# FFN down-projections as 2x2 block products in seven multiplications, summed over all block pairs in four PSUM banks

## The chip, the cores and the metric

One core of a Trainium2 chip runs the whole program. The metric is the time on the device in microseconds; shown are the median of three runs and the range, and one execution with a profile.

## The reference

A decoder trunk of two layers on `x` of 1024 rows by 1024 columns, in fp32. Layer 0 is a retention layer, layer 1 differential attention over keys and values that are projected once from the output of layer 0; each is followed by a ConvFFN with D_FF = 2816:

```python
def conv_ffn(xn, w_up, conv_w, conv_b, w_down):
    h = xn @ w_up                        # 1024 x 5632
    ...                                  # causal depthwise conv, width 3
    g, u = jnp.split(hc, 2, axis=-1)
    return (jax.nn.silu(g) * u) @ w_down # (1024 x 2816) @ (2816 x 1024)
...
h = conv_ffn(rms_norm(x, ffn_norm_pre[layer]), ...)
x = x + rms_norm(h, ffn_norm_post[layer])
```

The change concerns the last product, once in each layer.

## The kernel before

All large products keep fp32 accuracy by a split: a tile is rounded to fp32r (`hi`, a copy on ScalarE, L82), and the rest `lo` = tile − `hi` is taken on VectorE (L83); a product is then three matmuls, hi·hi, hi·lo and lo·hi (L98 to L100 in `mm3`, L511 in `gated`).

The stages follow one another on TensorE: retention to 0.5 ms, its gated output projection, FFN up of layer 0 (about 890 to 1342 us), FFN down of layer 0 (1342 to 1608), attention (1651 to 2120) with its output projection, FFN up of layer 1 (2200 to 2632) and FFN down of layer 1 (2633 to 2881).

FFN up (`ffn_up`) is already done as 2x2 block products in seven multiplications; its operands are split through a ring of eight 128x512 tiles `wc`. After convolution and SwiGLU each of the 22 blocks of 128 features goes to DRAM (`acts[f]`, 128 features by 1024 rows).

FFN down (`gated`) reads these blocks and those of `w_down` again (`load_w`: 512 KB, 128x1024, split into a tile `hl`), in groups of 1, then nine times 2, then 3 blocks. For each group and each of 8 blocks of 128 output rows it multiplies into a PSUM tile `ps` of two banks (128x1024), of which four rotate, and VectorE adds the tile to `acc` in SBUF (copy at L527, add at L529, last group L568). That is 22 blocks x 8 row blocks x 2 column halves x 3 = 1056 matmuls of 128x512 per layer.

With the last group the generator `finish` runs over the row blocks: mean square (ScalarE L110), reciprocal root (POOL L104, L105), gain (VectorE L169), residual (L173), and in layer 0 the normed rows for attention (ScalarE L205 `xhn`), their transposes (TensorE L121) and their split (`into_xt`). The first projections of attention (keys, queries, values of head pair 0) stand between the last transposes; their weights are loaded ahead and multiplied by a gain on POOL (L90).

The order of instructions on each engine is set by the program's text and a scheduler that works from it; loads are issued by SyncE (SP) in the order in which the text asks for them.

Of the kernel before, what the change touches and what calls it, by code (L numbers as in the profile page):

```python
# [50 lines left out]
def trunk(ctx: ExitStack, tc: tile.TileContext, A, out):  # L51
# [88 lines left out]
    def into_xt(ps, sb, xt):  # L140
        c, b = divmod(sb, 4)
        cols = slice(b * P, (b + 1) * P)
        if isinstance(xt, Staged):
            xt.put(ps, c, cols)
            return
        xh, xl = xt
        split_to(xh[c][:, :, cols], xl[c][:, :, cols], ps)

    def finish(mm, add, pool, psp, gpost, x_old, x_new, xt, order=tuple(range(NS)), turn_first=False, late=()):
# [82 lines left out]
        if xt is None:  # L232
            mm(NS - 1)
            halves = []
            for u in range(2):
                us = slice(u * 512, (u + 1) * 512)
                hs, t = add(NS - 1, u)
                hg = pool.tile([P, 512], F32, name="hg", tag="w4")
                halves.append((hg, t, mean_square(hs, D)))
                nc.vector.tensor_tensor(out=hg, in0=hs, in1=gpost[:, us], op=ALU.mult)  # L240
            r = small.tile([P, 1], F32, name="rstd")
            nc.gpsimd.tensor_scalar(out=r, in0=halves[0][2], scalar1=EPS, scalar2=halves[1][2],  # L242
                                    op0=ALU.add, op1=ALU.add)
# [254 lines left out]
    def gated(wk, up, n_blk, w_down, fin):  # L498
# [21 lines left out]
        def down(first, acts, ids, ws=None):  # L520
            ws = ws or [load_w(wk.hlp, w_down[i]) for i in ids]
# [12 lines left out]
        for gi, g in enumerate(sizes):  # L534
            ids = list(range(f, f + g))
            f += g
            acts, ws = [], []
            for u, i in enumerate(ids):
                acts.append(up(i))
                if wk.stored:  # L540
                    ws.append(load_w(wk.hlp, w_down[i]))
                if todo is not None and u == (g - 1 if wk.stored and g < 3 else 0):
                    down(*todo)
            todo = (gi == 0, acts, ids, ws)
        _, acts, ids, ws = todo
        ws = ws or [load_w(wk.hlp, w_down[i]) for i in ids]
# [29 lines left out]
    def open_mid(wk, tag, side):  # L576
        st = wk.mid = ExitStack()
        wk.accp = st.enter_context(tc.tile_pool(name="acc" + tag, bufs=8, side=side, reuse_waits="tile"))
        wk.w4 = st.enter_context(tc.tile_pool(name="w4" + tag, bufs=6, side=side, reuse_waits="tile"))
        wk.gp = st.enter_context(tc.tile_pool(name="gp" + tag, bufs=1, side=side, reuse_waits="tile"))  # L580
        open_junk(wk.gp, D)

    def open_ops(wk, tag, stored=0):
        st = wk.ops = ExitStack()
        wk.stored = stored
        wk.hlp = st.enter_context(tc.tile_pool(name="hlp" + tag, bufs=stored or 5, reuse_waits="tile"))
        if stored:
            return
        wk.actp = st.enter_context(tc.tile_pool(name="act" + tag, bufs=3, reuse_waits="tile"))
# [19 lines left out]
    def ffn_up(layer, xt, tail, w_pool, late, on_drained):  # L609
# [49 lines left out]
        ring = st.enter_context(tc.tile_pool(name=f"ring{layer}", bufs=8, reuse_waits="tile"))  # L659
# [104 lines left out]
        for f in range(NF):  # L764
# [43 lines left out]
            ready.extend(coming)  # L808
            cg = conv(f, hg)
# [22 lines left out]
    open_mid(wk, "a", "left")  # L832
# [5 lines left out]
    xt3 = []  # L838

    def last(mm, add):  # L840
        xt3.append(new_xt(xtp))
        g = load_gain(wk.gp, "gpost", A["ffn_norm_post"][0])
        return finish(mm, add, wk.w4, psp, g, x1, x2, xt3[0])
# [4 lines left out]

    acts = ffn_up(0, xt, tail, wk.hlp, None, drained)
    open_ops(wk, "f", 8)  # L850
    open_mid(wk, "f", "left")
    tail = gated(wk, stored(wk, acts), NF, rows(A["w_down"][0], NF), last)
    xt = xt3[0]

# [4 lines left out]
    gq, gkv = gains4[:, 0, :], gains4[:, 1, :]  # L859
# [29 lines left out]
    def load_v(pool, p):  # L889
        gv = gkv.rearrange("p (a k) -> p a k", a=2)  # L890
        return [load_w(pool, A["w_kv_v"][p, kh], gv[:, kh, :]) for kh in range(2)]

    wkq = [load_w(wk.hlp, A["w_kv_k"][0], gkv), load_w(wk.hlp, A["w_q"][0], gq)]
    wv = load_v(wk.hlp, 0)
    pkq = []
    for w in wkq:
        next(tail)
        pkq.append(psp.tile([P, S], F32, name="ps"))
        proj_half(pkq[-1][:, :512], w, 0)
    next(tail)  # L900
    pv = psp.tile([P, 4, 256], F32, name="ps")
    for sb in range(4):
        proj_v(pv[:, sb, :], wv, xt, sb)
    for _ in tail:
        pass
    wk.mid.close()
    qkp = qk4.enter_context(tc.tile_pool(name="qk4", bufs=2, side="right", reuse_waits="tile"))
# [17 lines left out]
    split_to(vs[0][0][:, :4, :], vs[0][1][:, :4, :], pv)  # L925
    ps_pool.close()
# [315 lines left out]
    def last(mm, add):  # L1242
        g = load_gain(wk.gp, "gpost", A["ffn_norm_post"][1])
        return finish(mm, add, wk.w4, psp, g, x3, x_out, None)

    acts = ffn_up(1, xt, tail, o5, late, drained)
    open_ops(wk, "b", 9)
    open_mid(wk, "b", "right")
    tail = gated(wk, stored(wk, acts), NF, rows(A["w_down"][1], NF), last)
    for _ in tail:  # L1250
        pass
    wk.mid.close()
    wk.ops.close()
    ps_pool.close()
# [69 lines left out]
```

## Time and profile before

| | |
|---|---|
| median of 3 runs | 2894.06 us (2892.62 to 2896.27) |
| profiled execution | 2892.49 us, span 2890.7 us |
| mean granted TensorE clock | 0.988 |
| busy in the span | TensorE 96%, VectorE 66%, ScalarE 38%, POOL 13% |

A TensorE that is busy 96% of the span leaves two sources of time: fewer matmuls, and the few places where it waits.

### The profile page before, as it was taken

Reading aid. Unit: us, or ns where it says so; the run is one execution under the profiler, and the core shown is the slowest. Engines: PE = TensorE matmul, PEld = TensorE weight load, DVE = VectorE, ACT = ScalarE, POOL = GpSimd, SP = SyncE. Lnnn points to the kernel's source line nnn. Section 1 sums busy time; section 2 is a strip of 40 time slices with the busy share of each in tenths; the row PEclk is TensorE's granted clock in tenths of the full one; section 3 lists DMA queues with packets and bytes.
Section 4 is the critical chain, followed back from the end, with each engine's and each line's share of the span. In section 5 each row is a group of like instructions: output and inputs, shape, how many; then the busy total and the mean of one; then the engine's idle time right before and its main releaser. Section 6 shows DMA issues by size and latency. Waiting matters only on the chain. (4 is left out here: it accounts for less than half of the span.)

```text
span 2890.7 us, 35455 instructions
## 1 busy us (share of the span) xinstructions
PE 2779.6 (96%) x13924; PEld 2344.9 (81%) x13924; DVE 1903.4 (66%) x2474; ACT 1098.9 (38%) x1776; POOL 372.8 (13%) x594
## 2 busy tenths in 40 slices
PE   8999999999997899999998999999989899999998
PEld 7888989888886688887887788888777788887887
DVE  4432333444448898887766587777648898887666
ACT  3323232311125344443212555555545344443212
POOL 1110111000012000000002334444421000000002
PEclk9999999999998999999999999999999999999999
DMA  4111120311222222223323323223252222224332
GB/s 142 55 48 59 38 65 27 133 69 66 81 102 88 87 96 88 82 79 138 110 90 121 122 73 80 75 68 94 86 177 100 90 100 75 86 80 160 110 102 95
DMA packets 102359, 262.89 MB, mean 91 GB/s; under 512 B 11440, under 2 KB 37040, under 8 KB 102192
## 3 DMA queue, kind: packets, MB, share of 16 engines
q1 hardware_dynamic: 72224, 210.03, 21.7%
q10 hardware_dynamic: 29968, 50.60, 5.0%
q8 instruction: 109, 1.79, 0.2%
q14 instruction: 58, 0.48, 0.0%
HBM read 193.48 MB, written 54.53 MB: 86 GB/s over the span
## 5 line engine op out<-in xcount | busy, mean ns | idle before, releaser
L511 PE MATMUL ps<-hl 128*128 128x512 f32 x2112 | 487.9, 392 | 11.5 <-DVE acc L527 3.8
L511 PEld LDWEIGHTS ps<-hl 128*128 128x128 f32 x2112 | 397.6, 189 | 100.3 <-DVE acc L527 7.3
L82 ACT ACTIVATE hl<-raw 128x1024 fp32r<-128x1024 f32 x190 | 198.7, 1056 | 625.1 <-PE ps L511 319.4
L83 DVE TENSOR_TENSOR hl<-raw,hl 128x1024 fp32r<-128x1024 f32 x190 | 239.6, 1262 | 143.2 <-ACT hl L82 142.6
L529 DVE TENSOR_TENSOR acc<-ps,acc 128x1024 f32<-128x1024 f32 x192 | 234.0, 1221 | 127.2 <-PE ps L511 126.3
L98 PE MATMUL ps<-xh,hl 128*128 128x512 f32 x592 | 233.2, 394 | 2.6 <-DVE xl L83 2.4
L99 PE MATMUL ps<-xl,hl 128*128 128x512 f32 x592 | 232.0, 392 | 3.2 <-DVE xl L83 3.2
L100 PE MATMUL ps<-xh,hl 128*128 128x512 f32 x592 | 232.2, 392 | 0.0
L104 POOL TENSOR_SCALAR rstd<-ss 128x1 f32<-128x1 f32 x127 | 56.7, 447 | 1177.3 <-ACT junk L110 1172.0
L511 PE MATMUL ps<-hl,act 128*128 128x512 f32 x768 | 178.4, 392 | 0.0
L759 DVE SCALAR_TENSOR_TENSOR hbuf<-hbuf,cw,hbuf 128x1023 f32<-128x1023 f32 x124 | 156.8, 1279 | 19.5 <-ACT hbuf L757 18.6
L511 PEld LDWEIGHTS ps<-hl,act 128*128 128x128 f32 x768 | 144.1, 189 | 29.5
L83 DVE TENSOR_TENSOR wc<-raw,wc 128x512 fp32r<-128x512 f32 x208 | 140.9, 685 | 37.0 <-ACT wc L82 37.0
L82 ACT ACTIVATE wc<-raw 128x512 fp32r<-128x512 f32 x208 | 128.6, 627 | 85.6 <-PE pb L100 77.2
L90 POOL TENSOR_TENSOR raw<-raw,gains 128x1024 f32<-128x1024 f32 x32 | 66.9, 2094 | 704.0 <-DMA raw<-in_w_kv_k 662.5
L98 PE MATMUL ps<-hl,xh 128*128 128x256 f32 x544 | 154.9, 286 | 1.8 <-ACT xh L82 1.8
L100 PE MATMUL ps<-hl,xl 128*128 128x256 f32 x544 | 155.4, 286 | 0.8 <-DVE xl L83 0.7
L99 PE MATMUL ps<-hl,xh 128*128 128x256 f32 x544 | 154.8, 285 | 0.0
L757 ACT ACTIVATE hbuf<-hbuf,cw 128x1024 f32<-128x1024 f32 x88 | 109.4, 1245 | 96.1 <-DVE hbuf L731 85.5
L1013 ACT ACTIVATE s<-s,m 128x256 f32<-128x256 f32 (+7 forms) x128 | 99.1, 774 | 101.2 <-POOL m L1012 100.8
L99 PEld LDWEIGHTS ps<-xl,hl 128*128 128x128 f32 x592 | 111.9, 189 | 26.9 <-DVE xl L83 4.1
L98 PEld LDWEIGHTS ps<-xh,hl 128*128 128x128 f32 x592 | 112.0, 189 | 26.4 <-DVE xl L83 2.6
(252 smaller groups left out, 6584.3 us busy)
## 6 DMA issues: line engine op xcount, KB each, us to landing
raw<-in_w_up SPq DMA_DIRECT2D x88, 512.0 KB, 3.5
act<-hbuf ACTq DMA_DIRECT2D x44, 512.0 KB, 2.6
raw<-act SPq DMA_DIRECT2D x44, 512.0 KB, 3.2
raw<-in_w_down SPq DMA_DIRECT2D x44, 512.0 KB, 3.5
raw<-in_w_t SPq DMA_DIRECT2D x32, 512.0 KB, 3.5
xold<-x SPq DMA_DIRECT2D x24, 512.0 KB, 5.1
raw<-in_w_v SPq DMA_DIRECT2D x16, 512.0 KB, 3.5
oret<-t ACTq DMA_DIRECT2D x32, 256.0 KB, 2.3
```

The source lines that it names most:

```text
L82: nc.scalar.activation(out=hi, in_=src, func=AF.Copy)
L83: nc.vector.tensor_tensor(out=lo, in0=src, in1=hi.bitcast(F32), op=ALU.subtract)
L90: nc.gpsimd.tensor_tensor(out=v, in0=v, in1=gain.unsqueeze(2).broadcast_to([P, gain.shape[1], n]), op=ALU.mult)
L98: nc.tensor.matmul(out, sh, mh, start=start, stop=False, skip_group_check=onto)
L99: nc.tensor.matmul(out, sh, ml, start=False, stop=False, skip_group_check=onto)
L100: nc.tensor.matmul(out, sl, mh, start=False, stop=stop, skip_group_check=onto)
L104: nc.gpsimd.tensor_scalar(out=r, in0=ss, scalar1=1.0, scalar2=eps, op0=ALU.mult, op1=ALU.add)
L511: nc.tensor.matmul(ps[:, half, :], a, ws[f][:, m, hs], start=f == 0 and n == 0, stop=f == len(ws) - 1 and n == 2)
L529: nc.vector.tensor_tensor(out=acc[sb], in0=flat(ps), in1=acc[sb], op=ALU.add)
L757: nc.scalar.activation(out=hc, in_=src, func=AF.Identity, scale=cw[:, n, 2:3], bias=cw[:, n, 3:4])
L759: nc.vector.scalar_tensor_tensor(out=hc[:, j:], in0=src[:, :S - j], scalar=cw[:, n, 2 - j:3 - j], in1=hc[:, j:], op0=ALU.mult, op1=ALU.add)
L1013: nc.scalar.activation(out=s[:, :w], in_=s[:, :w], func=AF.Exp, scale=0.125, bias=m, accum_out=l[:, c:c + 1])
```

## The change

FFN down becomes the class `Down`. Rows are cut into two halves of 512 and columns into two halves of 512; the 22 blocks of features make N = 11 pairs. For each pair the 2x2 by 2x2 product is formed by seven products P1 to P7 of 512x128 by 128x512, in place of eight. The loop over the products is the outer one: P1, P7, P5, P4, P6, P3, P2, each summed over all 11 pairs in four PSUM banks (one for each 128 rows), `px` or `py`. A step (one product, one pair) is 4 x 3 = 12 matmuls of 128x512, so a layer has 7 x 11 x 12 = 924. P5 and P3 go on top of what `px` holds, P4 on top of P7 in `py`. Only after a product is a bank copied (ScalarE) or added (VectorE) into `acc`.

Operands are loaded as halves (256 KB, rows of 2 KB), kept in SBUF as fp32 (`keep...`), combined on VectorE for P7, P5, P4 (two operations per step) and P6, P3 (one), and split through the ring `wc`. Loads are asked for 6 steps ahead, operands prepared 3 steps ahead. Rows 0 to 3 are complete after P6, so `finish` runs on them under P3 and P2; the last 4 pairs of P2 are done row block by row block, for rows 4 to 7. The last row block takes its column half 1 first. The first weights of attention (`load_first`) are asked for ahead of the last row block.

```diff
+    def minus(out, x, y):
+        nc.vector.tensor_tensor(out=out, in0=x, in1=y, op=ALU.subtract)
...
-            for u in range(2):
+            for u in (1, 0):
                 us = slice(u * 512, (u + 1) * 512)
                 hs, t = add(NS - 1, u)
...
+            if f == NF - 1:
+                down = Down(layer, acts, split_part, xt.pool)
+                for _ in range(4):
+                    down.load()
+                for _ in range(3):
+                    down.prepare()
...
+        N = NF // 2
+        ORDER = [(p, i) for p in ("P1", "P7", "P5", "P4", "P6", "P3", "P2") for i in range(NF // 2)]
+        LOADED, SPLIT = 6, 3
+        BY_ROWS = 4
...
+        def load(self):
+            p, i = self.ORDER[self.loaded]
+            a, b = self.a, self.b
+            if p == "P1":
+                self.fetch(self.a11(i), a(1, 1, i))
+                self.raw[p, i] = self.two(rawp, lambda j: b(1, 1, j), i)
+            elif p == "P7":
+                for dst, src in ((self.s(i), a(2, 1, i)), (self.t(i), b(1, 2, i)), (self.v(i), b(2, 2, i))):
+                    self.fetch(dst, src)
+            elif p == "P5":
+                self.raw[p, i] = self.halves(self.w4, a(2, 2, i), b(1, 1, i))
+            elif p == "P4":
+                self.raw[p, i] = self.halves(self.w4, a(2, 2, i), b(2, 1, i))
...
+        def prepare(self):
+            p, i = self.ORDER[self.split]
+            raw = self.raw.pop((p, i), None)
+            if p == "P1":
+                x, y = self.a11(i), raw
+            elif p == "P7":
+                d = self.w4.tile([P, 1024], F32, name="d", tag="w4")
+                x, y = d[:, COLS[0]], d[:, COLS[1]]
+                minus(x, self.a11(i), self.s(i))
+                minus(y, self.v(i), self.t(i))
+            elif p == "P5":
+                x, y = self.s(i), self.t(i)
+                nc.vector.tensor_tensor(out=x, in0=x, in1=raw[:, COLS[0]], op=ALU.add)
+                minus(y, y, raw[:, COLS[1]])
+            elif p == "P4":
+                x, y = raw[:, COLS[0]], raw[:, COLS[1]]
+                minus(self.t(i), self.v(i), self.t(i))
+                minus(y, y, self.t(i))
+            elif p == "P6":
+                x, y = self.s(i), self.t(i)
+                minus(x, x, self.a11(i))
+            elif p == "P3":
+                x, y = raw, self.v(i)
+                minus(x, x, self.s(i))
+            else:
+                x, y = self.s(i), raw
+            self.ops[p, i] = self.split_part(x), self.split_part(y)
+            self.split += 1
+        def ahead(self, p, i):
+            at = self.ORDER.index((p, i))
+            while self.loaded < min(at + 1 + self.LOADED, len(self.ORDER)):
+                self.load()
+            while self.split < min(at + 1 + self.SPLIT, len(self.ORDER)):
+                self.prepare()
+        def products(self, p, i, banks, js=range(4), onto=False):
+            (ah, al), (bh, bl) = self.ops[p, i]
+            for j in js:
+                m = slice(j * P, (j + 1) * P)
+                mm3(banks[j], ah[:, m], al[:, m], bh, bl, not onto and i == 0, i == self.N - 1, onto)
+        def full(self, p, banks, pairs=None, onto=False):
+            for i in pairs or range(self.N):
+                self.ahead(p, i)
+                self.products(p, i, banks, onto=onto)
...
+            def copy(dst, src):
+                for d, b in zip(dst, src):
+                    nc.scalar.activation(out=d, in_=b, func=AF.Copy)
+            def plus(dst, src, u=None):
+                for d, b, o in zip(dst, src, u or dst):
+                    nc.vector.tensor_tensor(out=d, in0=b, in1=o, op=ALU.add)
+            x = [self.bank_x() for _ in range(4)]
+            y = [self.bank_y() for _ in range(4)]
+            self.full("P1", x)
+            copy(c(1, 1), x)
+            self.full("P7", y)
+            copy(c(2, 2), y)
+            self.full("P5", x, onto=True)
+            plus(c(2, 2), x)
+            self.full("P4", y, onto=True)
+            plus(c(2, 1), y, c(1, 1))
+            self.full("P6", y)
+            plus(c(2, 1), y)
+            plus(c(2, 2), y)
+            copy(c(1, 2), y)
+            g = fin(self.mm, self.add)
+            self.acc, self.x = acc, x
+            self.c12 = lambda: plus(c(1, 2), x)
+            n = self.N - self.BY_ROWS
+            self.steps = [("P3", i) for i in range(self.N)] + [("P2", i) for i in range(n)]
+            return g
+        SIZES = (2, 4, 4, 4, 4)
+        def mm(self, sb):
+            if sb < 5:
+                for _ in range(self.SIZES[sb]):
+                    p, i = self.steps.pop(0)
+                    if p == "P3":
+                        self.full(p, self.x, [i], True)
+                        if i == self.N - 1:
+                            self.c12()
+                            self.on_p3()
+                    else:
+                        if i == 0:
+                            self.last = [self.bank_y() for _ in range(4)]
+                        self.full(p, self.last, [i])
+            if sb >= 4:
+                for i in range(self.N - self.BY_ROWS, self.N):
+                    self.ahead("P2", i)
+                    self.products("P2", i, self.last, [sb - 4])
+        def add(self, sb, half):
+            a = self.acc[sb]
+            if sb >= 4 and half != 1:
+                nc.vector.tensor_tensor(out=a[:, COLS[0]], in0=self.last[sb - 4], in1=a[:, COLS[0]], op=ALU.add)
+            if half is not None:
+                a = a[:, COLS[half]]
+            return a, a
...
+    def load_first():
+        first_w.extend((load_w(wk.hlp, A["w_kv_k"][0], gkv), load_w(wk.hlp, A["w_q"][0], gq), load_v(wk.hlp, 0)))
```

VectorE where FFN down of layer 0 begins (`hbuf` and `u` belong to the last block of FFN up, whose results leave PSUM at L731; `hl` are the split operands of FFN down). Before:

```order
L731 TENSOR_TENSOR hbuf_7081<-pb,u 128x512 x2
L759 SCALAR_TENSOR_TENSOR hbuf_7082<-hbuf_7081,cw,hbuf_7082 128x1023
L731 TENSOR_TENSOR hbuf_7082<-pb,u 128x512
L759 SCALAR_TENSOR_TENSOR hbuf_7082<-hbuf_7081,cw,hbuf_7082 128x1022
L83 TENSOR_TENSOR hl<-raw,hl 128x1024 x2
```

and now (L735 is the old L731, L763 the old L759, `wc` are split operands of P1):

```order
L83 TENSOR_TENSOR wc<-keepl,wc 128x512
L735 TENSOR_TENSOR hbuf_7081<-pb,u 128x512
L83 TENSOR_TENSOR wc<-raw,wc 128x512
L83 TENSOR_TENSOR wc<-keepl,wc 128x512
L83 TENSOR_TENSOR wc<-raw,wc 128x512
L83 TENSOR_TENSOR wc<-keepl,wc 128x512
L83 TENSOR_TENSOR wc<-raw,wc 128x512
L735 TENSOR_TENSOR hbuf_7082<-pb,u 128x512
```

The splits of the first three steps stand ahead of the last result of FFN up, where the first split of before stood behind it and behind two convolution steps.

VectorE between P7 and P5 of layer 0, which is new (`d` and L119 are differences, L912 the sum of P5, `wc<-d` the split of P7):

```order
L119 TENSOR_TENSOR d<-keeps 128x512
L119 TENSOR_TENSOR d<-keepvh,keeph 128x512
L83 TENSOR_TENSOR wc<-d,wc 128x512 x2
L912 TENSOR_TENSOR keeps<-keeps,raw 128x512
L119 TENSOR_TENSOR d<-keeps 128x512
L119 TENSOR_TENSOR d<-keepvl,keepl 128x512
L119 TENSOR_TENSOR keeph<-keeph,raw 128x512
L83 TENSOR_TENSOR wc<-d,wc 128x512 x4
```

Differences for later steps stand ahead of the splits of earlier ones.

VectorE near the end of FFN down of layer 0, rows 4 and 5. Before:

```order
L568 TENSOR_TENSOR acc<-ps,acc 128x1024
L169 TENSOR_TENSOR acc<-acc,gpost 128x1024
L173 SCALAR_TENSOR_TENSOR acc<-acc,rstd,xold 128x1024
L83 TENSOR_TENSOR xl_11267<-ps,xh_11265 128x8x128
L568 TENSOR_TENSOR acc<-ps,acc 128x1024
```

and now (L179 is the old L169, L183 the old L173, L1025 the add of P2; `hl` are the weights of attention):

```order
L1025 TENSOR_TENSOR acc<-py,acc 128x512
L83 TENSOR_TENSOR hl<-raw,hl 128x1024
L179 TENSOR_TENSOR acc<-acc,gpost 128x1024
L83 TENSOR_TENSOR hl<-raw,hl 128x1024
L183 SCALAR_TENSOR_TENSOR acc<-acc,rstd,xold 128x1024
L83 TENSOR_TENSOR xl_11257<-px,xh_11256 128x4x128 x2
L1025 TENSOR_TENSOR acc<-py,acc 128x512
L83 TENSOR_TENSOR hl<-raw,hl 128x1024
L179 TENSOR_TENSOR acc<-acc,gpost 128x1024
L83 TENSOR_TENSOR xl_11257<-px,xh_11256 128x4x128
L183 SCALAR_TENSOR_TENSOR acc<-acc,rstd,xold 128x1024
```

The add is half as wide, and the splits of the attention weights have moved in between.

## Rows read from the trace of the kernel before

**Rows 1.** The page: busy time (share of the span) of each engine, instructions.

```profile
PE 2779.6 (96%) x13924; PEld 2344.9 (81%) x13924; DVE 1903.4 (66%) x2474; ACT 1098.9 (38%) x1776; POOL 372.8 (13%) x594
```

**Rows 2.** FFN down of layer 0: L511's matmuls, with first and last start.

```profile
L511 PE MATMUL ps<-hl x876: 388/389/390, 1371.7 to 1570.0; 128*128 128x512 f32 x176
```

**Rows 3.** Busy us (instructions) by stretch; columns in the first line.

```profile
core 0: us, PE busy (x) PEld busy (x) DVE busy (x) ACT busy (x) POOL busy (x), PEclk, DMA share, GB/s
...
1342.00:1372.00 30.00, 25.39 (x93) 18.50 (x92) 24.91 (x23) 8.92 (x9) 0.00 (x0) 0.89 0.54 197
2632.00:2660.00 28.00, 21.07 (x83) 15.12 (x84) 22.79 (x21) 8.67 (x9) 0.00 (x0) 1.00 0.58 211
1570.00:1655.00 85.00, 69.27 (x365) 58.82 (x364) 52.19 (x53) 46.17 (x64) 37.82 (x39) 0.92 0.41 139
1060.00:1330.00 270.00, 270.00 (x1193) 223.59 (x1192) 230.18 (x299) 125.82 (x169) 0.00 (x0) 1.00 0.24 84
```

**Rows 4.** What TensorE waited for, 1342 to 1372 us.

```profile
PE ps L511 <- DVE acc L527: 1.9, 2, 1.5
PE ps L511 <- DVE hbuf L731: 1.4, 1, 1.4
PE ps L511 <- DVE hl L83: 1.3, 1, 1.3
```

**Rows 5.** What TensorE waited for, 2630 to 2662 us.

```profile
PE ps L511 <- ACT hl L82: 3.0, 2, 1.7
...
PE ps L511 <- DVE hl L83: 1.8, 2, 1.4
```

**Rows 6.** What TensorE waited for, 1572 to 1655 us.

```profile
PE ps L121 <- ACT xhn L205: 13.4, 3, 9.6
PE ps L98 <- DVE xl L83: 2.4, 1, 2.4
```

**Rows 7.** The page's groups: the 128x512 splits, busy and mean ns; POOL's gains.

```profile
L83 DVE TENSOR_TENSOR wc<-raw,wc 128x512 fp32r<-128x512 f32 x208 | 140.9, 685 | 37.0 <-ACT wc L82 37.0
L82 ACT ACTIVATE wc<-raw 128x512 fp32r<-128x512 f32 x208 | 128.6, 627 | 85.6 <-PE pb L100 77.2
L90 POOL TENSOR_TENSOR raw<-raw,gains 128x1024 f32<-128x1024 f32 x32 | 66.9, 2094 | 704.0 <-DMA raw<-in_w_kv_k 662.5
```

**Rows 8.** Timeline of VectorE in FFN up: start, duration.

```profile
1304.80 0.68 DVE L731 TENSOR_TENSOR hbuf<-pb,u 128x512 f32<-128x512 f32 x1
1305.40 0.68 DVE L83 TENSOR_TENSOR wc<-raw,wc 128x512 fp32r<-128x512 f32 x1
```

**Rows 9.** Timeline of layer 0's tail: one row's chain.

```profile
1581.68 1.41 POOL L105 TENSOR_TENSOR rstd<-rstd,mhalf 128x1 f32<-128x1 f32 x1
1583.12 1.15 ACT L205 ACTIVATE xhn<-acc,rstd 128x1024 f32<-128x1024 f32 x1 [3.00 <-POOL rstd L105]
...
1584.03 1.28 DVE L173 SCALAR_TENSOR_TENSOR acc<-acc,rstd,xold 128x1024 f32<-128x1024 f32 x1 [1.35 <-POOL rstd L105]
...
1589.84 1.06 ACT L110 ACTIVATE junk<-acc 128x1024 bf16<-128x1024 f32 x1 [1.44 <-DVE acc L568]
```

**Rows 10.** Timeline of the program's end.

```profile
2879.19 1.52 PE L511 MATMUL ps<-hl 128*128 128x512 f32 x6
...
2886.03 1.41 DVE L248 SCALAR_TENSOR_TENSOR acc<-hg,rstd,xold 128x512 f32<-128x512 f32 x2 [0.45 <-POOL rstd L244]
```

**Rows 11.** DMA, 1342 to 1372 us, in 40 slices.

```profile
GB/s 0 55 339 350 404 388 399 404 421 393 415 393 235 0 0 11 0 0 82 410 208 0 0 93 377 229 0 0 126 350 246 240 284 142 11 22 147 366 153 191
```

**Rows 12.** What TensorE waited for, 880 to 980 us.

```profile
PE pb L98 <- DVE hbuf L731: 6.7, 2, 4.5
PE pb L100 <- DVE wc L83: 4.9, 2, 4.5
```

**Rows 13.** DMA, 1372 to 1570 us, in 40 slices.

```profile
GB/s 113 180 131 187 214 3 0 170 157 97 5 103 165 156 0 0 215 196 16 0 123 194 109 0 48 170 206 0 3 191 148 84 0 105 168 156 0 0 212 32
```

More of the change, by code (lines that the diff above doesn't have):

```diff
@@ L518, in flat, with down @@
             return ps.rearrange("p a b -> p (a b)")
-        def down(first, acts, ids, ws=None):
-            ws = ws or [load_w(wk.hlp, w_down[i]) for i in ids]
+        def down(first, acts, ids):
+            ws = [load_w(wk.hlp, w_down[i]) for i in ids]
             for sb in range(NS):
@@ L607, in ret_up, with ffn @@
         return up
-    def ffn_up(layer, xt, tail, w_pool, late, on_drained):
+    def ffn(layer, xt, tail, w_pool, late, on_drained, wk, fin):
         N_PRE = 6
@@ L837, in trunk, with open_half @@
     xt = nxt
-    xt3 = []
+    xt3 = [None, None], [None, None]
+    def open_half(c):
+        for part, n in zip(xt3, "hl"):
+            part[c] = xtp.tile([P, NK, 512], F32R, name=f"x{n}{c}", tag=f"x{n}{c}")
     def last(mm, add):
-        xt3.append(new_xt(xtp))
         g = load_gain(wk.gp, "gpost", A["ffn_norm_post"][0])
-        return finish(mm, add, wk.w4, psp, g, x1, x2, xt3[0])
+        open_half(0)
+        down = mm.__self__
+        down.on_p3 = lambda: open_half(1)
+        return finish(mm, add, wk.w4, down.bank_x, g, x1, x2, xt3, late=(load_first,))
     def drained():
@@ L847, in drained, with load_v @@
         wk.ops.close()
[L849 to L853, printed above, removed]
+    first_w = []
+    def load_first():
+        first_w.extend((load_w(wk.hlp, A["w_kv_k"][0], gkv), load_w(wk.hlp, A["w_q"][0], gq), load_v(wk.hlp, 0)))
+    gq, gkv = gains4[:, 0, :], gains4[:, 1, :]
+    def load_v(pool, p):
+        gv = gkv.rearrange("p (a k) -> p a k", a=2)
+        return [load_w(pool, A["w_kv_v"][p, kh], gv[:, kh, :]) for kh in range(2)]
+    tail, order = ffn(0, xt, tail, wk.hlp, None, drained, wk, last)
+    xt = xt3
     HALF = (slice(0, 64), slice(64, 128))
@@ L886, in proj_half @@
             mm3(ps, w[:, 0, ws], w[:, 1, ws], xh[c][:, k, :], xl[c][:, k, :], k == 0, k == NK - 1)
[L889 to L899, printed above, removed]
-    next(tail)
-    pv = psp.tile([P, 4, 256], F32, name="ps")
+    pkq, pv = [], []
+    next(tail)
+    bank_x, bank_y = wk.down.bank_x, wk.down.bank_y
+    wkq, wv = first_w[:2], first_w[2]
+    for u, w in enumerate(wkq):
+        if u:
+            next(tail)
+        pkq.append(bank_y())
+        proj_half(pkq[-1], w, 0)
+    next(tail)
     for sb in range(4):
-        proj_v(pv[:, sb, :], wv, xt, sb)
+        if sb % 2 == 0:
+            pv.append(bank_y().rearrange("p (j n) -> p j n", n=256))
+        proj_v(pv[-1][:, sb % 2, :], wv, xt, sb)
     for _ in tail:
@@ L1243, in last @@
         g = load_gain(wk.gp, "gpost", A["ffn_norm_post"][1])
[L1244 to L1249, printed above, removed]
+        mm.__self__.on_p3 = lambda: None
+        return finish(mm, add, wk.w4, None, g, x3, x_out, None)
+    tail, order = ffn(1, xt, tail, o5, late, drained, wk, last)
     for _ in tail:
         pass
+    order.close()
     wk.mid.close()
+    wk.ring.close()
     wk.ops.close()
-    ps_pool.close()
+    wk.banks.close()
 def layout(inputs):
```

129 lines of the change are left out of this document (92 added, 37 removed).

## The prediction

> **What bounds the kernel now.** First the page's engine shares: TensorE is busy 2779.6 of 2890.7 us [rows 1], so a change counts by the matmuls it removes and by TensorE's waits. Then L511's matmuls in the down stage: 876 starts from 1371.7 to 1570.0 us [rows 2] are (1570.0 − 1371.7)/875 = 0.2266 us from start to start, with no wait in them; the 0.39 us that a row shows for one is its length in the pipeline, not its price. Then the windows [rows 3], where 0.2266 us per start tells what a stretch loses: 1342 to 1372 us holds 93 starts, 21.1 us, and so loses 8.9 us; 2632 to 2660 us holds 83, 18.8 us, and loses 9.2. These are the two places where FFN down takes over from FFN up. The waits name the cause: the last results of FFN up, the splits `hl` and the first copies into `acc` [rows 4, 5]. In layer 0 the granted clock is 0.89 there, in layer 1 it is 1.00 [rows 3]. Last the tail of layer 0, where TensorE waits 13.4 us for `xhn` and 2.4 us for a split [rows 6], at a mean clock of 0.92 [rows 3]. Between the levels of 2.4 GHz (1) and 1.2 GHz (one half), a mean of 0.92 over 85 us is 13.6 us at the lower; 9.6 us of that can lie in the longest wait, and in the other 4.0 half the work is lost, 2.0 us. The tail loses about 13.4 + 2.4 + 2.0 = 17.8 us.
>
> **The change part by part**, against the profiled execution's own 2892.5 us (1.8 us of it around the span of 2890.7), which is 1.6 us under the median.
>
> Matmuls: 2 x (1056 − 924) = 264 fewer, of the same shape, at 0.2266 us [rows 2]: −59.8 us.
>
> What feeds them: a step of 12 matmuls lasts 2.72 us. In P7, P5 and P4 VectorE has two differences and two splits per step, four 128x512 operations. One takes 685 ns alone [rows 7], but two neighbours in a queue start 0.60 us apart [rows 8]: 2.4 us (by the lone length 2.74 us). That is 88% of the step. In FFN up VectorE is busy 230.18 of 270 us, 85%, and TensorE has 1193 starts in those 270 us, 0.2263 us each: no loss [rows 3]. So the price is nothing as long as the orders keep VectorE from waiting for ScalarE, whose two splits of 627 ns [rows 7] are 1.25 us per step. In the order of P7 and P5 differences for later steps stand ahead of earlier splits, which covers ScalarE. If that cover is gone, it is the first rival. I take the back-to-back value, since queues are full there.
>
> The adds into `acc` disappear from the steady state: of 88 per layer over two banks remain nine rounds over four single banks. Most leave time: P5 goes onto `px` and P4 onto `py` without any read in between. P6 starts in the very banks that P4 leaves, and each has to be read by VectorE first: 0.69 us for the first, while splits of two steps stand ahead of it in that queue; the other three follow at 0.60 us, and TensorE needs 0.68 us for a bank's three matmuls. From 0.7 to 2.5 us per layer. Under P3, VectorE also holds P6's eight adds and the first rows of `finish`: 1.8 us of each 2.72 for the steps, 4.8 us of adds, 2.6 us per row (residual 1.28 [rows 9], the gain taken to be as long), which the three steps of lead can just hold. No row of before shows these. From below the price is nothing, from above 10 us per layer (a wait of the size of the longest in the tail, 9.6 us [rows 6], at one of the places). I take +5 us for both layers, nearer to the short waits of 1.3 to 1.7 us that such handovers cost in rows 4 and 5.
>
> The start of FFN down: the first three steps are split ahead of the last results of FFN up, and the first copy out of a bank comes after 11 steps, so all three waits of rows 4 and 5 have lost their cause. What is late next is the handover of PSUM from `pb` to `px`, with a read of the last product by VectorE ahead of it. I leave about 1 us each: 18.1 − 2 = −16 us (bounds 0 and −18).
>
> Tail of layer 0: rows 0 to 3 are finished under P3 and P2, so their `xhn` come early, and only rows 4 to 7 follow each other at 12 matmuls, 2.72 us. One row's chain: add 0.69 (as a split [rows 7]), square 1.06, POOL's root up to 1.41, residual 1.28, a second square and root, `xhn` 1.15 [rows 9]: up to 9.5 us with the summing and handovers left out. After the last matmul of FFN down TensorE has 24 matmuls for the keys, 24 for the queries and 96 of half width for the values, some 22 us, ahead of the first product that needs row 7. The keys need row 3's split, whose second half stands on VectorE behind row 5's residual and a weight split. Row 5's last matmul is 5.4 us before the stage's end; add 0.7, square 1.1, root 1.4, residual 1.3, a 128x1024 split that I take as long as the residual, 1.3, and the split's half 0.7 make 6.5, and with 0.3 to 2 for handovers 6.8 to 8.5: late by 1.4 to 3. On POOL the reciprocal roots stand behind the gain multiplications of the attention weights, 2.09 us each [rows 7], which wait for their loads: another 0 to 6 us if these come late. I leave 7 of 17.8 us: −11 (bounds −17 and 0).
>
> Tail of layer 1: six matmuls stand from 2879.19 for 1.52 us, to 2880.7, and VectorE's last piece ends at 2886.03 + 1.41 = 2887.4 [rows 10], 6.7 us later. Now half 1 of the last row is complete before P2, and only a half add, square, root and residual follow: −2.
>
> Loads: P7 needs three of 256 KB per step, 786 KB per 2.72 us or 290 GB/s; the other products need two at most, 193. Before, 339 to 421 GB/s lasted for ten slices of 0.75 us [rows 11], with whole 512 KB loads. I take no cost. The Trainium skill, page "DMA: Bandwidth & Descriptors", section "Bandwidth", says to batch DMAs to 1 MiB or more, since smaller ones reach less than three quarters of the peak; the change halves them. From its times for 64 KB (0.95 us) and 1 MB (6.15 us) I estimate 2.0 us for 256 KB, and 6.0 us per P7 step if the three came one by one, +72 us over 22 steps. Rows 11 speak against that rule here: several half-megabyte loads in flight ran at 339 to 421 GB/s.
>
> Start of FFN up: the ring of split operands now lies elsewhere, and the order of splits there changes a little: the splits for the X21 products come after those of two more operands. TensorE waits there 6.7 us and 4.9 us for VectorE already [rows 12]. Between 0 and +5; I take +2.5.
>
> Sum: −59.8 + 5 − 16 − 11 − 2 + 2.5 = −81.3, 2811.2 by the profiled execution, 2813 for the median.
>
> **Rivals.**
> 1. Slower: each step's chain runs without overlap, difference, ScalarE split, VectorE split. In P7, P5 and P4 it is 2 x 0.685 + 2 x 0.627 + 2 x 0.685 = 4.0 us [rows 7], +1.28 over 2.72 for 33 steps in each of two layers, +84; in P6 and P3 3.3 us, +0.6 x 44 = +26. Then 2813 + 110 = 2923. It undoes the gain when the heavy chain passes about 3.7 us. For it: VectorE is within 12% of the step. Against it: the lead of three steps, the order, and FFN up at 85%.
> 2. P7 is bound by its loads. Busiest slices in the old down stage reach 215 GB/s [rows 13], though there on demand; at that rate a step takes 3.7 us, +0.95 x 22 = +21: 2834. For it: rows of 2 KB in place of 4 KB. Against it: rows 11, and six steps of lead. The Trainium skill's batching rule (same page and section) names this mechanism.
> 3. Only the arithmetic is gained: both starts lose 18 us again and the tail 18, at other places: 2892.5 − 59.8 + 7.5 = 2840, 2842 for the median. For it: each place hands PSUM over between engines, as before. Against it: the new orders.
> 4. The change does not do what it says, the matmuls stay at 1056: TensorE's order shows 924, so this is next to excluded.
>
> **How the numbers follow.** My forecast has 0.72, its own range 2801 to 2826; only the arithmetic 0.12, P7's loads 0.10, slower 0.05, nothing changed 0.01. The range 2799 to 2843 holds the first three and leaves out the rest and some of the forecast's edges. About 0.2% is what a measurement of this kernel tells from no change: 6 us. Faster 0.94, within 0.2% 0.01, slower 0.05.
>
> **What would show it.** 1848 matmuls of L98 to L100 into `px` and `py`, 0.227 us apart within P1, P7, P5, P4; VectorE busy near 88% in P7 to P4; a wait of about 1 us at P4 to P6 and at the first `px`; a wait of 1 to 8 us before the keys' projection; VectorE's end 5 us after the last matmul. Regular waits for `wc` in every step would mean rival 1; waits for a DMA into `keep` tiles in P7 rival 2; waits of 8 us or more at the starts rival 3.

## The result, and the profile after

The changed kernel takes 2850.02 us (median of four runs, 2848.21 to 2852.5) against 2895.16 us (2892.62 to 2896.85) before: ratio 0.9845, 95% interval 0.9828 to 0.9862. The span fell by 41.0 us to 2849.7 us. The forecast was 2813 us, −81.3, with a range from 2799 to 2843: almost half of the gain is missing, and the time lies above the range.

The page after, beside [rows 1]: TensorE is busy 37.5 us less, although 59.8 us of matmuls went.

```profile
span 2849.7 us, 35674 instructions
...
PE 2742.1 (96%) x13660; PEld 2298.3 (81%) x13660; DVE 1919.2 (67%) x2750; ACT 1193.4 (42%) x2029; POOL 370.6 (13%) x594
```

So busy time itself became longer somewhere, and that shows only in windows (columns as in [rows 3]). The first and last lines are FFN up, whose text did not change; the others are P1, P7, P5, P4, P6 and P3 of layer 0, cut near their first matmuls (P1's is at 1351.8), and the tail.

```profile
1060.00:1330.00 270.00, 270.00 (x1159) 217.66 (x1158) 224.50 (x292) 122.40 (x167) 0.00 (x0) 1.00 0.22 80
1351.00:1386.40 35.40, 32.27 (x138) 25.23 (x137) 25.53 (x38) 16.18 (x28) 0.00 (x0) 1.00 1.04 382
1386.40:1417.10 30.70, 30.20 (x133) 24.68 (x132) 30.70 (x52) 16.05 (x30) 0.00 (x0) 1.00 0.54 186
1417.10:1449.00 31.90, 30.62 (x134) 24.62 (x133) 31.90 (x54) 13.34 (x24) 0.00 (x0) 1.00 0.32 110
1449.00:1481.00 32.00, 30.64 (x134) 24.70 (x133) 26.89 (x45) 12.79 (x22) 0.00 (x0) 1.00 0.52 181
1481.00:1511.00 30.00, 30.00 (x133) 24.62 (x132) 16.44 (x27) 12.70 (x22) 0.00 (x0) 1.00 0.10 36
1511.00:1542.60 31.60, 30.18 (x133) 24.70 (x132) 29.73 (x44) 21.46 (x38) 7.21 (x10) 1.00 0.60 208
1546.00:1630.00 84.00, 74.34 (x392) 63.13 (x392) 53.16 (x68) 48.22 (x77) 34.59 (x31) 0.96 0.45 149
2320.00:2580.00 260.00, 260.00 (x1123) 209.99 (x1122) 217.60 (x282) 120.37 (x161) 0.00 (x0) 1.00 0.23 83
```

FFN up of layer 0 holds 1159 starts in the same 270 us where before had 1193 [rows 3], at a full clock, with TensorE busy throughout: each matmul takes 233.0 ns (270/1159) instead of 226.3. (A window counts every matmul that touches it, so the quotients are 0.1 to 0.2% low; from start to start it is 233.3 and 226.7.) It costs 9.6 us up to the end of the stage. Layer 1 has 260/1123 = 231.5 ns, before 260/1138 = 228.5:

```profile
2320.00:2580.00 260.00, 260.00 (x1138) 213.23 (x1137) 222.58 (x291) 123.09 (x168) 0.00 (x0) 1.00 0.24 85
```

That stage became 3.4 us longer. In FFN down 132 matmuls of a product at 0.2267 us are 29.92 us; what a product lasts beyond that is its loss. P1 loses most (4.6 us in layer 0, 5.5 in layer 1), and DMA is at 382 GB/s for its whole length. In P7 and P5 VectorE is busy in every microsecond of the stretch. The longest single loss, 6.1 us, is in P3 of layer 1; its window, and what TensorE waited for in it:

```profile
2774.70:2810.70 36.00, 31.89 (x134) 25.79 (x132) 31.32 (x46) 18.17 (x34) 5.72 (x8) 0.95 0.62 220
```

```profile
PE px L99 <- DVE wc L83: 4.1, 1, 4.1
```

The waits at the start of layer 0's FFN down, then at layer 1's, where [rows 4, 5] stood:

```profile
PE px L98 <- ACT wc L82: 2.0, 2, 1.6
PE px L99 <- DVE wc L83: 1.1, 3, 0.6
```

```profile
PE px L98 <- ACT wc L82: 3.1, 1, 3.1
PE px L99 <- DVE wc L83: 0.2, 1, 0.2
```

The old releasers, `hbuf` and `acc`, are gone. These rows add up to 6.4 of the 10.1 us that P1 loses in both layers from start to start. The new releaser is the split of an operand (`wc`), and the loads that SyncE issued ahead of P1's own, the DMA slices of 1351 to 1387 us and the groups of loads (last: KB, median us from issue to landing) tell why the split is late:

```profile
1348.53 3.45 SPq L866 DMA_DIRECT2D keeph<-in_w_down  x7
```

```profile
GB/s 246 271 339 369 376 398 401 403 401 394 389 380 398 385 382 394 385 378 396 382 387 391 401 416 391 403 396 382 391 394 382 373 389 392 394 391 387 389 378 391
...
keeps<-act SPq DMA_DIRECT2D x17, 256.0 KB, 5.4
...
raw<-in_w_down SPq DMA_DIRECT2D x7, 256.0 KB, 5.8
```

Against the ten busy slices of [rows 11] this is a plateau without a gap; on SyncE seven loads of `keeph` for P7 stand ahead of P1's own. The Trainium skill ("DMA: Bandwidth & Descriptors", section "Bandwidth") expects less than three quarters of the peak from loads under 1 MiB and gives 435 GB/s as ceiling; its times are of loads issued by GpSimd. Here loads of 256 KB issued by SyncE, several in flight, ran at 382 GB/s, 88% of that ceiling, so the trace does not agree. What P1 lacked was not larger loads; whether it was the rate or the order of the loads, `p1_order` shows below.

The tail of layer 0, beside [rows 6], and the last VectorE work of the program, beside [rows 10]:

```profile
PE px L128 <- ACT xhn L215: 7.1, 1, 7.1
PE pj L98 <- DVE vl L83: 2.1, 1, 2.1
```

```profile
2845.04 1.41 DVE L258 SCALAR_TENSOR_TENSOR acc<-hg,rstd,xold 128x512 f32<-128x512 f32 x2 [0.45 <-POOL rstd L254]
```

The longest wait for `xhn` fell from 9.6 to 7.1 us, their sum from 13.4 to 7.1. TensorE waits these 7.1 us ahead of the fourth group of eight transposes, which is row 3 (the expectations below call it row 2). In the built program these are row 3's residual, row 4's sum, row 4's first mean square, row 3's second and row 3's `xhn`:

```profile
1556.14 1.29 DVE L183 SCALAR_TENSOR_TENSOR acc<-acc,rstd,xold 128x1024 f32<-128x1024 f32 x1 [0.72 <-POOL rstd L105]
...
1567.83 0.68 DVE L1025 TENSOR_TENSOR acc<-py,acc 128x512 f32<-128x512 f32 x1
...
1569.18 1.04 ACT L110 ACTIVATE junk<-acc 128x1024 bf16<-128x1024 f32 x1
...
1572.53 1.04 ACT L110 ACTIVATE junk<-acc 128x1024 bf16<-128x1024 f32 x1
...
1578.70 1.13 ACT L215 ACTIVATE xhn<-acc,rstd 128x1024 f32<-128x1024 f32 x1
```

Row 3 is ready at 1557.4 us, but `finish` writes its second mean square behind row 4's first, which needs row 4's sum; so it starts only 15 us later.

| term | predicted | measured |
|---|---|---|
| 264 matmuls | −59.8 | −59.8 |
| FFN up | +2.5 | +13.0 (9.6 + 3.4) |
| attention, to FFN up of layer 1 | 0 | +5.1 (561.8 us, 556.7 before) |
| start of FFN down | −16 | −8.0 (10.1 us lost in P1 stand for 18.1) |
| inside, P7 to P3 | +5 | +17.8 (P7 1.1, P5 4.5, P4 4.0, P6 0.4, P3 7.8, both layers) |
| tail of layer 0 | −11 | −7.3 (13.6 lost, 20.9 before, both from start to start) |
| tail of layer 1 | −2 | −1.1 (9.2 us from the last matmul to the end, 10.3 before) |
| sum | −81.3 | −40.3; the spans differ by 41.0 |

Attention's text did not change. No run takes its +5.1 apart, but with all tiles moved alike (`left64`, below) attention and FFN up of layer 1 together take 980.1 us, as before, and 988.7 in the changed kernel.

### The profile page after: what moved, and what is told of

It reads as the page before. It is cut to its first block, busy times and chain, and to the rows that moved or that the text cites. A ratio compares the mean times of both kernels' runs of the same rounds, so it can differ in the third digit from the quotient of the medians.

```text
span 2849.7 us, 35674 instructions
## 1 busy us (share of the span) xinstructions
PE 2742.1 (96%) x13660; PEld 2298.3 (81%) x13660; DVE 1919.2 (67%) x2750; ACT 1193.4 (42%) x2029; POOL 370.6 (13%) x594
## 5 line engine op out<-in xcount | busy, mean ns | idle before, releaser
L82 ACT ACTIVATE wc<-raw 128x512 fp32r<-128x512 f32 x318 | 195.3, 626 | 209.2 <-PE pb L100 86.6
L83 DVE TENSOR_TENSOR wc<-raw,wc 128x512 fp32r<-128x512 f32 x318 | 214.2, 684 | 60.6 <-ACT wc L82 60.6
L82 ACT ACTIVATE hl<-raw 128x1024 fp32r<-128x1024 f32 x102 | 107.5, 1056 | 293.5 <-PE ps L100 150.6
L99 PE MATMUL ps<-xl,hl 128*128 128x512 f32 x560 | 219.2, 391 | 3.3 <-DVE xl L83 3.3
L98 PE MATMUL ps<-xh,hl 128*128 128x512 f32 x560 | 219.9, 393 | 0.2 <-ACT hl L82 0.2
L100 PE MATMUL ps<-xh,hl 128*128 128x512 f32 x560 | 218.8, 391 | 0.0
L83 DVE TENSOR_TENSOR hl<-raw,hl 128x1024 fp32r<-128x1024 f32 x102 | 134.1, 1317 | 85.2 <-ACT hl L82 85.0
L763 DVE SCALAR_TENSOR_TENSOR hbuf<-hbuf,cw,hbuf 128x1023 f32<-128x1023 f32 x124 | 156.6, 1279 | 16.8 <-ACT hbuf L761 15.9
L98 PE MATMUL ps<-hl,xh 128*128 128x256 f32 x512 | 145.8, 286 | 1.7 <-ACT xh L82 1.7
L100 PE MATMUL ps<-hl,xl 128*128 128x256 f32 x512 | 146.4, 286 | 0.8 <-DVE xl L83 0.7
L99 PE MATMUL ps<-hl,xh 128*128 128x256 f32 x512 | 145.8, 285 | 0.0
L99 PE MATMUL py<-wc 128*128 128x512 f32 x352 | 138.5, 393 | 3.2 <-DVE wc L83 3.2
L98 PE MATMUL py<-wc 128*128 128x512 f32 x352 | 138.3, 393 | 0.0
L100 PE MATMUL py<-wc 128*128 128x512 f32 x352 | 137.7, 391 | 0.0
L98 PE MATMUL pb<-xh,wc 128*128 128x512 f32 x304 | 121.3, 399 | 7.9 <-ACT u L680 4.3
L100 PE MATMUL pb<-xh,wc 128*128 128x512 f32 x304 | 120.8, 397 | 7.3 <-DVE wc L83 7.3
```

The costliest lines, as they stand in the source:

```text
L82: nc.scalar.activation(out=hi, in_=src, func=AF.Copy)
L83: nc.vector.tensor_tensor(out=lo, in0=src, in1=hi.bitcast(F32), op=ALU.subtract)
L98: nc.tensor.matmul(out, sh, mh, start=start, stop=False, skip_group_check=onto)
L99: nc.tensor.matmul(out, sh, ml, start=False, stop=False, skip_group_check=onto)
L100: nc.tensor.matmul(out, sl, mh, start=False, stop=stop, skip_group_check=onto)
L763: nc.vector.scalar_tensor_tensor(out=hc[:, j:], in0=src[:, :S - j], scalar=cw[:, n, 2 - j:3 - j], in1=hc[:, j:], op0=ALU.mult, op1=ALU.add)
```

## The experiments

Each starts from the changed kernel if nothing else is said; ratios are to the kernel before, timed on the same chip.

**FFN up: the place of the ring.** In the built programs the ring's tiles begin at 32 modulo 128 bytes in layer 0 before, as do the other split operands; after, the ring begins at 96, the others in layer 0 still at 32; in layer 1 the tiles of `x` stand at 96 before and after. Theory A: a matmul is slower when its two operands stand 64 bytes apart modulo 128. Rivals: B, VectorE's new order; C, the DMA. `ring64` moves the ring by 64 bytes:

```diff
+        pad = wk.ring.enter_context(tc.tile_pool(name=f"pad{layer}", bufs=1, side="right", ...))
+        pad.tile([P, 16], F32, name="pad")
```

> The changed kernel with the ring of split operands moved down by 64 bytes per partition in both layers, nothing else. In the changed kernel the ring stands at a byte address of 96 modulo 128 and the moving operands of FFN up of layer 0 at 32; moved, both stand at 32. Theory A (a matmul is slower when its two operands differ by 64 bytes modulo 128): the matmuls of FFN up of layer 0 go from 0.2332 us back to 0.2267 us apart, -9 us; in layer 1 those on the tiles t1 to t4 and x22 (at 32) go to about 0.227 while those on x (at 96) become slow, as in the kernel before, -3 us; about 2837 us in all. Theory B (the ring is slow because it lies at the upper end of SBUF, or other engines' traffic slows TensorE): the distances stay at 0.232 to 0.233 us and the time at 2850.

Measured: 2837.2 us, 0.9804 (0.9789 to 0.9818). The window of layer 0 has its 1193 starts again:

```profile
1060.00:1330.00 270.00, 270.00 (x1193) 223.58 (x1192) 230.19 (x299) 125.97 (x169) 0.00 (x0) 1.00 0.25 84
```

In the built program every engine has the same instructions in the same order as in the changed kernel, so B falls, and the transfers are the same too: the place of the ring is the cause. `left64` moves the others instead, ahead of all left-hand tiles:

```diff
+    const.tile([P, 16], F32, name="pad")
     ident = const.tile(...)
```

> The changed kernel with 64 bytes per partition of padding below all tiles on the left side of SBUF, nothing else: all left tiles move to 96 modulo 128, where ring and right side stand. Theory A: all matmuls of FFN up in both layers at 0.2267 us, -9.4 us in layer 0 and -7 us in layer 1, about 2834 us; other stages that mix tiles of the two sides may gain too. Theory B: no change, 2850 us.

Measured: 2834.11 us, 0.9789 (0.9774 to 0.9804); layer 1 is whole as well, 260/1149 = 226.3 ns, where even the kernel before has only 1138 starts in that window:

```profile
2320.00:2580.00 260.00, 260.00 (x1149) 215.29 (x1148) 220.96 (x288) 122.69 (x165) 0.00 (x0) 1.00 0.25 85
```

`before_ring64` does the reverse in the kernel before: a pad of 64 bytes ahead of its ring and one behind it.

> The kernel before with its ring moved up by 64 bytes (and the tiles above it by 128, so that only the ring changes its place modulo 128). Theory A: FFN up of layer 0 goes from 0.2266 to 0.233 us per matmul, +9 to +10 us; in layer 1 the tiles t1 to t4 and x22 become slow and x fast, +3 to +5 us; about 2908 us. Theory B: no change, 2894 us.

Measured: 2901.21 us, 1.0023 (1.0013 to 1.0033), slower as A says, but by half of what it expected:

```profile
1060.00:1330.00 270.00, 270.00 (x1176) 220.50 (x1175) 227.65 (x297) 124.19 (x169) 0.00 (x0) 1.00 0.25 84
```

Here single matmuls range from 226 to 236 ns. A holds in its direction, but not as a rule for single pairs. In layer 1 of the kernel before, ring and tiles t at 32 and x at 96, the steps follow each other so (twelve matmuls from line to line):

```profile
2332.46 0.39 PE L98 MATMUL pb<-t1h,wc 128*128 128x512 f32 x1
...
2335.18 0.40 PE L98 MATMUL pb<-xh,wc 128*128 128x512 f32 x1
...
2337.95 0.40 PE L98 MATMUL pb<-t4h,wc 128*128 128x512 f32 x1
...
2340.72 0.39 PE L98 MATMUL pb<-x22h,wc 128*128 128x512 f32 x1
```

A step on t1 takes 2.72 us, the one on x 2.77, and the one on t4 behind it 2.77 too, though both of its operands stand at 32. What the runs show is that a stage goes at 226.7 ns where all its tiles stand alike, and slower where they are mixed; which matmul pays, and how much, is not settled. `before_left64` puts the pad of `left64` into the kernel before:

> The kernel before with the same 64 bytes of padding on the left side. Theory A: layer 0 of FFN up keeps its 0.2266 us (all its tiles are on the left), in layer 1 the tiles t and x now agree with x on the right: 0.2287 to 0.2266 us, -3 to -4 us, about 2891 us. So at equal alignment the change would be worth 2834 against 2891, 57 us.

Measured: 2891.27 us, 0.9983 (0.9974 to 0.9992), and layer 1 has 1149 starts too. So with aligned operands the change itself is worth about −56 us by the two ratios (0.9789/0.9983; the two kernels ran on different chips).

**P1: who has the DMA.** `store_pool` issues the store of the last block of FFN up from POOL. Theory C: that store holds up ScalarE's queue, and the splits of P1 behind it are late. Theory D: the loads themselves are late.

```diff
-            nc.scalar.dma_start(out=acts[f], in_=cg)
+            (nc.gpsimd if f == NF - 1 else nc.scalar).dma_start(out=acts[f], in_=cg)
```

> The changed kernel with only the store of the last feature block of FFN up issued from POOL's queue in place of ScalarE's. In the changed kernel ScalarE stands still for 5.4 us (1362.9 to 1368.3 us) and 5.9 us (2627.3 to 2633.2) at that store, which waits for a load that shares its semaphore, and the splits of P1's steps 6 to 8 are late by 4.6 and 5.4 us. Theory C (the store holds ScalarE's queue): the waits in P1 fall from 4.6 and 5.4 us to under 1.5 each, about 2843 us. Theory D (the loads themselves are late, since DMA runs at 382 GB/s for the whole of P1): the waits move by under 2 us in all, 2848 to 2850 us.

Measured: 2850.41 us, 0.9848 (0.9833 to 0.9863), no change; P1 loses 7.25 and 4.55 us in place of 4.6 and 5.5, in its steps 7 and 8. C falls. `p1_order` (on `left64`) holds SyncE to the program's order through P1 and P7:

```diff
+            with tc.manual_schedule(engines={mybir.EngineType.SP}):
                 self.full("P1", x)
                 copy(c(1, 1), x)
                 self.full("P7", y)
```

> left64 (all tiles aligned alike) with SyncE's order pinned to the program's text in P1 and P7 of both layers: P1's loads go ahead of those of P7, where in left64 seven loads for P7 (keeph) stand ahead of P1's. Theory F (P1's operands queue behind P7's, which are not due for 15 us): P1's waits fall from 4.8 and 6.1 us to under 1.5 each, P7's stay under 1; about -8 us against left64, 2826 us. Theory D (DMA is full at 382 GB/s, so bytes that go first only delay others): the sum of the waits in P1 and P7 stays at 5.7 and 6.4 us, 2834 us.

Measured: 2829.15 us, 0.9773 (0.9757 to 0.9789), an interval that overlaps that of `left64`. P1 and P7 do not wait at all, in either layer:

```profile
1341.00:1371.00 30.00, 30.00 (x134) 24.86 (x133) 25.26 (x37) 17.71 (x30) 0.00 (x0) 1.00 0.85 295
```

So F holds in P1 and P7, and this D falls: the loads were late because of their order, not because their bytes exceed what the DMA moves. P1 now runs at 295 GB/s, and P1 and P7 of layer 0 together move 18.5 MB, 19.1 in `left64`. But of the 12.0 us that P1 and P7 lost in `left64` only about 5 show in the time: P5 now loses 4.5 and 4.35 (1.9 and 2.6 there) and P3 2.5 more, while P4 loses 1.6 less. (With SyncE pinned, the scheduler also moved operations on VectorE.) P5's window:

```profile
1401.00:1435.00 34.00, 31.77 (x132) 25.49 (x131) 34.00 (x58) 13.29 (x24) 0.00 (x0) 0.95 0.37 123
```

VectorE runs 58 operations here, of which P5 needs 44: P4's differences, ready early, stand ahead of P5's splits.

**VectorE's order.** `pre_order` (on `p1_order`) queues the sums and differences of a step behind the splits of the step two before:

```diff
+            if len(self.los) > 1 and p != "P1":
+                behind.enter_context(tc.issue_after(self.los[-2]))
             ...                      # the sums and differences of the step
+            behind.close()
             self.ops[p, i] = self.split_part(x), self.split_part(y)
+            self.los.append(marks["split"].ins)
```

> p1_order with the sums and differences of each step queued on VectorE behind the splits of the step two before, in place of the scheduler's order, in which those of P4 stand ahead of P5's splits. Theory H (TensorE waits in P5 and P4 because VectorE, full at 34.0 of 34.0 us, does P4's differences before the splits that are due): the waits in P5 and P4 fall from 5.4 and 5.8 us to under 1.5 in each layer, -8 to -9 us against p1_order, 2820 us. Rival 1 of the prediction in this place (difference, ScalarE split, VectorE split run one after another when the order is not free): the waits grow, above 10 us per layer, over 2835 us.

Measured: 2813.9 us, 0.9718 (0.9702 to 0.9734), more than H expected. P1, P7, P5 and P4 lose 0.0 us in both layers, and P5 has air:

```profile
1401.00:1431.00 30.00, 30.00 (x134) 24.84 (x133) 27.73 (x46) 13.87 (x25) 0.00 (x0) 1.00 0.55 171
```

VectorE's 27.73 of 30.00 us is 92%, near the 88% of the prediction. What remains is 0.8 us at P4 to P6, P3's 2.6 and 4.8, and the tail.

**P3 in layer 1.** `pace1` (on `left64`) queues gain and residual of a finished row behind the splits already asked for, and gives layer 1 more steps of P3 before the first row; the run does not separate the two:

```diff
-                for _ in range(self.SIZES[sb]):
+                for _ in range((self.SIZES, (6, 3, 3, 3, 3))[self.layer][sb]):
...
-                    residual(a)
+                    with tc.issue_after(marks["split"].ins) if xt is None else ExitStack():
+                        residual(a)
```

> left64 with VectorE's finishing work of rows 0 to 3 (gain and residual) in layer 1 queued behind splits of later steps, row by row from P3's sixth step on into P2, where it all stands ahead of P3's eighth step in left64. Theory G (VectorE is overfull in P3, the finishing rows stand ahead of the splits that TensorE waits for): the wait of 5.8 us in P3 of layer 1 falls under 1, -5 us, 2829 us. Rival (the two raw buffers let P3's loads come late): the wait stays above 4 us, 2833 to 2834.

Measured: 2826.04 us, 0.9761 (0.9746 to 0.9775); P3's loss in layer 1 goes from 6.07 to 0 us.

**The tail of layer 0.** `v_late` (on `left64`) puts the load and gain of the values' weights behind row 3's `xhn` and root, so that POOL is free for the roots:

```diff
-        first_w.extend((..., load_v(wk.hlp, 0)))
+    with tc.issue_after(marks["xhn", 3].ins), tc.issue_after(marks["pow", 3].ins):
+        wv = load_v(wk.hlp, 0)
```

> left64 with the weights of the values (loads, POOL gain, splits) issued behind row 3's xhn on ScalarE and its root on POOL, in layer 0's tail. Theory E (ScalarE's queue holds the normed row 2 behind the split of those weights, which waits for a late load and POOL): TensorE's wait ahead of row 2's transposes falls from 7.1 us to 3 or 4, -3 to -4 us, 2830 us. Rival (row 2's own chain over ScalarE, POOL and VectorE is that long): under 1 us, 2833 to 2834.

Measured: 2831.02 us, 0.9778 (0.9763 to 0.9792), which the interval of `left64` overlaps. The wait for `xhn`, 7.6 us in `left64`, becomes 4.2, but another of 2.8 us for `xhn` appears behind it, and the values' first product waits 2.8 in place of 2.1, and the way from FFN up's end to attention's first product stays at 274.3 us. `no_gain` (on `all`, next) leaves out the gain multiplications of these weights:

```diff
-        first_w.extend((load_w(wk.hlp, A["w_kv_k"][0], gkv), load_w(wk.hlp, A["w_q"][0], gq), load_v(wk.hlp, 0)))
+        first_w.extend((load_w(wk.hlp, A["w_kv_k"][0]), load_w(wk.hlp, A["w_q"][0]), ...))
```

> all without POOL's four gain multiplications of the first attention weights (keys, queries, values of head 0): these weights go unscaled into their splits, and nothing else is left out. Theory K (POOL's multiplications of 1.9 us each, in a queue with the reciprocal roots, and the VectorE splits beside them, 2.77 and 2.33 us in place of 1.21, set layer 0's tail): TensorE's wait ahead of row 2's transposes falls from 7.1 us to under 4 and the way from FFN up's end to attention's first matmul from 266.4 to about 262 us; 2804 us. Rival (the rows' own chain): within 1 us of all, 2807 to 2809 us.

Measured: 2808.16 us, 0.9699 (0.9682 to 0.9715), the same as `all`, 2808.35. The waits for `xhn` in `all`, then in `no_gain`:

```profile
PE px L130 <- ACT xhn L221: 7.1, 1, 7.1
```

```profile
PE px L130 <- ACT xhn L221: 7.6, 2, 5.3
```

That POOL's gains make the tail late is therefore false. What `no_gain` keeps of the changed kernel is the order of the mean squares: row 3's (1555.90 us) comes on ScalarE behind row 4's (1552.85), whose sum VectorE adds at 1552.08. No run took that order apart, so that it sets the wait is read from the traces and not shown.

**All together.** `all` is `left64`, `p1_order`, `pre_order` and `pace1`; `all_v` adds `v_late`.

> left64, p1_order, pre_order and pace1 together. If the four causes are separate: waits from P1 to P3 under 3 us in each layer, only the tail of layer 0 left; 2834 - 5 - 8 - 6 = 2815 us. If each wait only hands VectorE's backlog on to the next product, as P1's gain partly went to P5 in p1_order: 2820 to 2826 us.

> all, with v_late's later weights of the values as well. In v_late the wait ahead of row 2 fell by 3.4 us but the way from FFN up's end to the first matmul of attention stayed at 274.3 us, since the later waits grew: so no difference to all, within 2 us.

Measured: `all` 2808.35 us (2807.14 to 2809.57), 0.9698 (0.9683 to 0.9712), the fastest of all, level with `no_gain`, which leaves work out. FFN down of layer 1 loses 1.4 us in all, and before P2 layer 0 keeps 3.4, most of it in P3. So the gains add up, and to 7 us more than the 2815 expected, since `pre_order` alone gave 15 us against `p1_order` where 8 had been put down. `all_v` 2812.47 us, 0.9713 (0.9697 to 0.9727): no gain, 4 us longer than `all` where at most 2 were expected.

## Why the prediction was wrong

It was right that 264 matmuls go at 0.2267 us, that the copies leave the start, that the handovers from `pb` to `px` and from P4 to P6 cost little (0 and 0.2 us; 0.8 in `pre_order`), and that VectorE has the capacity: with the orders mended it feeds P7, P5 and P4 without one wait. Rival 1, the unoverlapped chain, is thereby excluded. Four steps failed.

1. **"The ring of split operands now lies elsewhere … between 0 and +5"** (+2.5, measured +13.0). It saw that the ring moves and then priced the order of splits only. What counted was the address: 6.7 ns on each of over a thousand matmuls in layer 0, off in `ring64`, in part on in `before_ring64`. The order cost nothing: from its first to its last matmul the stage takes 422.1 us in `ring64`, 424.3 before and 432.0 in the changed kernel. A cost per instruction was bounded by the size of waits.
2. **"The price is nothing as long as the orders keep VectorE from waiting"** and the +5 for what lies inside (17.8). The prediction read the differences ahead of earlier splits as a cover for ScalarE. They are what delays the splits: VectorE was busy for all of P7 and P5, not for 88%. Undone in `pre_order` (P5, P4). Under P3 it took the three steps of lead to hold the finishing rows as well; P3 loses 7.8 us, and `pace1` takes away the 6.1 of layer 1.
3. **"I leave about 1 us each"** at the start of FFN down (10.1 in both). The lead of three steps was real, but the operands of step 6 and later come late, behind loads for P7. Loads were weighed by P7's 290 GB/s; the peak is in P1, where P7's loads run ahead to 382 GB/s. This is near rival 2's mechanism, but in another product and by the order of the loads: `p1_order` removes the wait with the same loads.
4. **"I leave 7 of 17.8 us"** in the tail (13.6, of 20.9 counted from start to start; the 17.8 was 3.1 short). What failed is "rows 0 to 3 are finished under P3 and P2, so their `xhn` come early": row 3's `xhn` comes at 1578.7 us, behind row 4's sum, and TensorE waits 7.1 us for it. The place that the prediction feared, the keys' projection, waits at most 0.2 us, and POOL's gains, its other reason, do not matter (`no_gain`).

The time of 2850 lies near rival 3's 2842, but not by its mechanism: the starts lose 10.1 us and not 18, no wait there reaches 8 us, and 17.8 us are lost inside. One slip in the working carries nothing: the pieces listed for one row's chain add up to 8.1 us, not 9.5.

With the first three mended (the second only in P5 and P4), `pre_order` takes 2813.9 us and `all` 2808.35. That these lie near the 2813 of the forecast does not make the forecast right for the kernel as changed, and is in part luck: the tail still loses as much as in the changed kernel; and a part of it, some 5 us by the ratio 0.9983 of `before_left64`, is a loss that the kernel before has too.

## What to carry to other kernels

When a change moves a pool, compare the starts in a window of unchanged, saturated work before looking for waits: a matmul that became 3% longer shows in no list of waits. Where an engine is at 88%, look in the order for work that stands ahead of what is due, and price it as a delay; a lead in steps protects only if the loads are issued in the order of need; and a row that is ready early helps only if its work does not stand in a queue behind a row that is late.

## What the runs showed of the hardware

Matmuls of 128x512 in FFN up stood 226.7 ns from start to start where all its operands lie at 32 (layer 0 before, `ring64`) or all at 96 modulo 128 bytes (`left64`, `before_left64`), and 233.3 ns in layer 0 of the changed kernel with one operand at 96 and the other at 32; in `before_ring64` the same mixture gave 230.0 ns in the mean. In mixed stages a matmul whose own two operands lie alike can be slow too (t4 above). Why is not known.

VectorE slows beside POOL. The same split of 128x1024 in the tail of the changed kernel, beside a gain multiplication and 4 us later, and what ran on POOL meanwhile:

```profile
1569.31 2.83 DVE L83 TENSOR_TENSOR hl<-raw,hl 128x1024 fp32r<-128x1024 f32 x1 [0.80 <-ACT hl L82]
...
1573.19 1.21 DVE L83 TENSOR_TENSOR hl<-raw,hl 128x1024 fp32r<-128x1024 f32 x1
```

```profile
1569.16 1.90 POOL L90 TENSOR_TENSOR raw<-raw,gains 128x1024 f32<-128x1024 f32 x1 [0.97 <-DMA raw<-in_w_q]
...
1571.14 1.05 POOL L104 TENSOR_SCALAR rstd<-ss 128x1 f32<-128x1 f32 x1
```

It takes 2.83 us in place of 1.21, and ends 1.08 us after the multiplication; two later ones, of 2.32 and 1.99 us, end 1.08 us after theirs as well. In `no_gain`, without the multiplications, the four splits of the tail take 1.21 to 1.23 us. POOL's single column takes 1.05 us beside the split and 0.19 at the end of the program. The Trainium skill ("GPSIMD Engine Reference", section "2. Architecture") says that POOL shares its SBUF ports with VectorE; the two times agree with that. That removing the multiplications changed nothing in the total shows that this stretch of VectorE was not the one that the tail waits for.
